# Taking GpSimd out of the attention stage of a bidirectional gated-recurrence and mixture-of-experts block

## The chip, the cores and the metric

The kernel runs on one core of a Trainium2 chip. A core has a matrix engine (TensorE, PE in the profile; PEld is its loading of weights), VectorE (DVE), ScalarE (ACT), GpSimd (POOL) and SyncE (SP), which here only issues transfers. Each engine works through its own list of instructions in order; the engines wait for each other by semaphores. The metric is the time of one execution on the device, in microseconds (us), as the median of several runs; lower is better.

## The reference

One block of a diffusion model works on 256 latent tokens and 256 context tokens, each 1024 wide, in fp32. Cut to what matters:

```
mod = silu(c) @ w_mod + b_mod               # 6 rows of 1024: sh1, sc1, g1, sh2, sc2, g2
h   = rms_norm(x) * (1 + sc1) + sh1         # the context gets rows of its own
q, i, f_fwd, f_bwd, og, u, v, ga, gb = split(h @ w_in)   # 9 sections of 1024
f   = lb + (1 - lb) * sigmoid(f_logit);  k = 1 - f
# gated recurrence, 8 heads x 128, forward and backward, in chunks of 64:
b   = cumsum(log f) in the chunk;  r = b[31];  e = b[63]
s_t = (q * exp(b - r)) . (k * exp(r - b)), masked
o   = s_t @ i + (q * exp(b)) @ S
S   = exp(e) * S + (k * exp(e - b))^T @ i
# S starts from the context:  S0 = sum_s (k * exp(tail))^T @ i,  tail = sum of log f behind s
y_a = rms_norm(o) * gnorm * silu(og)
y_b = chunk_mlp(gelu(u), gelu(v))
x   = x + g1 * ((sigmoid(ga) * (y_a @ w_a) + sigmoid(gb) * (y_b @ w_b)) @ w_out)
x   = x + g2 * top4_of_32_experts(rms_norm(x) * (1 + sc2) + sh2)
out = rms_norm(x) * final_g
```

## The kernel before

**Stages.** Up to about 60 us the kernel computes the first two modulation rows, normalizes the tokens and projects the values and both forget logits of the first two heads. From there to about 345 us runs the attention stage, with which the change deals: the remaining sections of the projection for the heads, and the recurrence. Then come the chunk MLP, the branch projections and the output projection (to some 490 us), and from there to the end the 32 experts, whose weights stream through the chip at over 400 GB/s.

**Projections.** They are done in fp32 by three matmuls: ScalarE writes the high part of a weight (`ghi`, L265), VectorE subtracts it (`glo`, L266), and TensorE adds high times high, high times low and low times high (L346, from `hh`, `hl`, `ghi`, `glo`). A granule of weights is 1024 x 256, one transfer of 1 MB.

**The ring.** Granules of `w_in` and the tiles of `w_mod` (1024 KB too: four rows of 128 times 512 columns) share three slots. SyncE's queue issues their transfers in order, and each waits until its slot is free.

**Modulation sums.** The rows `g1`, `sh2`, `sc2`, `g2` are needed only later. Each is computed in two halves of 512 columns (`mod_sums`, L206 to L229), each half in two steps: step 0 for the first four blocks of 128 rows of `w_mod`, step 1 for the other four. Step 0 was GpSimd's: one product of 128x2048 with the broadcast conditioning column (L215), a sum of 128x1024 (L216) and one of 128x512 (L221). Step 1 was and is VectorE's: four fused multiply-adds of 128x512 (L228). A matmul with ones then sums over the partitions (L248, tile `tp`).

**A head.** `decays` (L444 to L480) takes logarithms of the forget gates (ScalarE, L450), makes four scans on VectorE (L458: `bl` within chunks, `cu` over the context), the difference `d` to the chunk's middle (L467), and on ScalarE the exponentials: `e1` and `e2` of plus and minus `d`, `cu`, and the small tile `w` of chunk decays (L475). VectorE multiplies these to the queries (L477) and keys (L478, tile `lf`). GpSimd subtracted 1 from the context's gate (L452), set two elements of `cu` to zero (L455), copied the 16 columns that go into `w` (L470, L471) and multiplied the context's keys (L479). `states` makes the scores (L496, TensorE), masks them (VectorE), turns the keys (L506, copied by L507) and computes the chunks' sums U (L515 and L518, tiles `ua` and `ub`). `output` carries the states over the chunks: an addition (L529, VectorE) and a scaling by two columns (L530), forward on VectorE and backward on GpSimd, tile `ks`; then TensorE adds up the head's output (`o_ps`, L535 and L539). `finish` normalizes it (square sums on ScalarE; `rstd_of` on VectorE, L103 to L109, with the small tiles `nv`, `ni`, `ny`, `nt`; L553 writes `on`), turns it (L556, tile `tp` from `on`), multiplies it with the gate, and splits it into high and low.

**The order.** The heads go in pairs. While the projections of pair j run, the heads of pair j-1 are computed, interleaved as a string says:

```
ORDER = "x0 d0 y0 m0 d1 x1 m1 d2 x2 y1 x3 m2 d3 y2 m3 y3 d4"
```

Here `d0` to `d4` are the projections of pair j (values, silu of q, silu of the output gate, both forget gates), `x0` to `x3` and `y0` to `y3` are decays, states, output and finish of the two heads, and `m0` to `m3` are the steps of two halves of a modulation row (step 0 and step 1 of each). In the last round gates stand in the place of the projections. From the order so written the framework's scheduler makes each engine's list: it simulates a timeline with costs of its own and lets ready instructions go ahead, so an edit of one instruction's engine or size also moves others. The experts' part is ordered by hand and isn't touched.

Of the kernel before, what the change touches and what calls it, by code (L numbers as in the profile page):

```python
# [12 lines left out]
AF = mybir.ActivationFunctionType  # L13
OP = mybir.AluOpType
PSUM = bass.MemoryType.PSUM

P = 128
D = 1024
KT = 8
T = 256  # L20
# [6 lines left out]
def view(t, off, dims):  # L27
    return bass.AP(tensor=t.tensor, offset=t.offset + off, ap=[t.ap[0], *dims])
# [3 lines left out]
def kernel(  # L32
# [5 lines left out]
    ve, sc, te, gp = nc.vector, nc.scalar, nc.tensor, nc.gpsimd  # L38
# [120 lines left out]
    for h in range(2):  # L159
        b = slice(h * 64, h * 64 + 64)  # L160
# [41 lines left out]
    cs32 = late.tile([P, KT, 32], F32, name="cs32")  # L202
# [3 lines left out]
    def mod_sums(j, h):  # L206

        a = wk.tile([P, 512], F32, name="modrow")

        def step(k4):  # L210
            wt = wtile([P, 4, 512])
            nc.sync.dma_start(wt, w_mod[0, k4 * 512:(k4 + 1) * 512, j * D + h * 512:j * D + (h + 1) * 512]
                              .rearrange("(k p) n -> p k n", p=P))
            if k4 in MOD_POOL:
                gp.tensor_mul(wt, wt, cs32[:, 4 * k4:4 * k4 + 4, 0:1].to_broadcast([P, 4, 512]))  # L215
                gp.tensor_add(wt[:, 0:2], wt[:, 0:2], wt[:, 2:4])  # L216
                if k4:
                    gp.tensor_add(a, a, wt[:, 0])
                    gp.tensor_add(a, a, wt[:, 1])
                else:  # L220
                    gp.tensor_add(a, wt[:, 0], wt[:, 1])  # L221
            else:
                for q in range(4):
                    kt = 4 * k4 + q
                    if kt == 0:
                        ve.tensor_scalar(a, wt[:, q], cs32[:, kt, 0:1], None, op0=OP.mult)
                    else:
                        ve.scalar_tensor_tensor(a, wt[:, q], cs32[:, kt, 0:1], a, op0=OP.mult, op1=OP.add)  # L228
        return a, step  # L229

    def mod_col(j, h, res):
# [158 lines left out]
    for k in range(2):  # L390
        a, b = cols2[:, 8 + 16 * k:16 + 16 * k], cols2[:, 16 + 16 * k:24 + 16 * k]
# [51 lines left out]
    def decays(hd, k, q):  # L443


        col = slice(hd, hd + 1)
        lf = wk.tile([P, 2, 2 * T], F32, name="lf")
        tc.keep_in_program_order(sc.preload_act_table_set("natural_log_exp_and_others"))
        for dr in range(2):
            tc.keep_in_program_order(sc.activation(lf[:, dr], k[:, dr], AF.Ln, scale=omlb[dr][:, col], bias=lb[dr][:, col]))  # L450
        kl, kc = k[:, :, 0:T], k[:, :, T:2 * T]
        gp.tensor_scalar(kc, kc, -1.0, None, op0=OP.add)  # L452
        bl = wk.tile([P, 2, T], F32, name="bl")
        cu = wk.tile([P, 2, T], F32, name="cu")
        gp.memset(view(cu, T - 1, [[1, 2]]), 0.0)  # L455

        def scan(dst, o, src, so, m, n, st):
            ve.tensor_tensor_scan(view(dst, o, [[st, n]]), m, view(src, so, [[st, n]]), 0.0, op0=OP.mult, op1=OP.add)  # L458

        whole = view(reset, 1, [[0, T - 1]])  # L460
        scan(bl, 0, lf, 0, reset, T, 1)
        scan(bl, 2 * T - 1, lf, 3 * T - 1, reset, T, -1)
        scan(cu, T - 2, lf, 2 * T - 1, whole, T - 1, -1)
        scan(cu, T + 1, lf, 3 * T, whole, T - 1, 1)
        e1, e2 = lf[:, :, 0:T], lf[:, :, T:2 * T]
        d1 = wk.tile([P, 2, T], F32, name="d1")
        ve.tensor_sub(view(d1, 0, [[T, 2], [64, 4], [1, 64]]), view(bl, 0, [[T, 2], [64, 4], [1, 64]]),  # L467
                      view(bl, 31, [[T + 1, 2], [64, 4], [0, 64]]))
        w = wk.tile([P, 2, 2, 4], F32, name="w")
        gp.tensor_copy(w[:, 0], view(bl, 31, [[T + 1, 2], [64, 4]]))  # L470
        gp.tensor_copy(w[:, 1], view(d1, 63, [[T - 63, 2], [64, 4]]))  # L471
        sc.activation(e1, d1, AF.Exp)
        sc.activation(e2, d1, AF.Exp, scale=-1.0)
        sc.activation(cu, cu, AF.Exp)
        sc.activation(w, w, AF.Exp)  # L475
        for dr in range(2):
            ve.scalar_tensor_tensor(e1[:, dr], e1[:, dr], nomlb[dr][:, col], q, op0=OP.mult, op1=OP.mult)  # L477
        ve.scalar_tensor_tensor(e2, kl, -1.0, e2, op0=OP.add, op1=OP.mult)  # L478
        gp.tensor_mul(cu, cu, kc)  # L479
        return e1, e2, cu, w  # L480

    def attend(hd, dec, iv, og):
# [38 lines left out]
        def output():  # L521
            qt, w = dec[0], dec[3]
            sm, S, R, U, ua, ub = (st[k] for k in ("sm", "S", "R", "U", "ua", "ub"))
            sc.activation(S[:, 0, 0], ua[:, 3], AF.Copy, scale=w[:, 0, 0, 0:1])
            sc.activation(S[:, 1, 3], ub[:, 3], AF.Copy, scale=w[:, 0, 1, 3:4])
            for n in range(3):
                for dr, a, b in ((0, n, n + 1), (1, 3 - n, 2 - n)):
                    r = R[:, dr, b]
                    ve.tensor_add(r, S[:, dr, a], U[dr, a])  # L529
                    (gp if dr else ve).tensor_scalar(S[:, dr, b], r, w[:, 1, dr, a:a + 1], w[:, 0, dr, b:b + 1],  # L530
                                                     op0=OP.mult, op1=OP.mult)
            o = bank("o_ps", (P, 2, P))
            for tt in range(2):
                for dr in range(2):
# [518 lines left out]

ORDER = "x0 d0 y0 m0 d1 x1 m1 d2 x2 y1 x3 m2 d3 y2 m3 y3 d4"
FIRST = 6
MOD_POOL = (0,)
WARM = 20
WARM2 = (3, 12)
RING_A = 3
# [30 lines left out]
```

## Time and profile before

The rows are one profiled execution; the times are of runs without a profile.

| what | before |
|---|---|
| median of 3 runs | 1435.1 us |
| lowest and highest run | 1431.59 and 1438.36 us |
| profiled execution | 1439.14 us |
| its span | 1437.4 us |
| mean granted clock of TensorE | 0.978 |
| TensorE matmuls busy | 1341.1 us, 93% of the span |
| TensorE weight loads busy (beside matmuls) | 727.7 us, 51% |
| VectorE busy | 615.9 us, 43% |
| ScalarE busy | 306.2 us, 21% |
| GpSimd busy | 171.8 us, 12% |

The span is the time from the first to the last recorded instruction. Busy shares are averages over stages that differ, so a stage is read from rows for its own stretch of time. A row of the timeline begins with the start and the length of an instruction, both in us, then its engine, line, operation, result and sources, and behind x its number; in brackets stands the idle time of the engine just ahead of it, with what ended that. A row of the waits names who waited for whom: us in total, how often, and the longest. A row of a tile gives the shortest, middle and longest duration in ns. Granted clock 1.00 is TensorE's full speed.

### The profile page before, as it was taken

The page shows a single profiled execution, that of the slowest core. Times are in us where ns is not written, and L with a number is a line of the kernel's source. Part 1 is how long each engine was busy: PE and PEld are TensorE (multiplying, and loading weights), DVE is VectorE, ACT ScalarE, POOL GpSimd, SP SyncE. Part 2 cuts the span into 40 slices and gives each one's busy share as a digit, 9 for nine tenths or more (in the row PEclk, how much of TensorE's full clock was granted, in tenths as well). Part 3 has the DMA queues.
Part 4 walks back from the last instruction along what each step waited for, and adds up shares of the span by engine and source line. Part 5 has one row for each costly group of instructions (what it writes and reads, how often), then busy time and mean ns, then how long its engine had stood idle before and what let it go on. Part 6 is the DMA issues. An engine that isn't in the chain of part 4 may idle for free. (4 is left out here: it accounts for less than half of the span.)

```text
span 1437.4 us, 18504 instructions
## 1 busy us (share of the span) xinstructions
PE 1341.1 (93%) x7806; PEld 727.7 (51%) x7806; DVE 615.9 (43%) x1100; ACT 306.2 (21%) x494; POOL 171.8 (12%) x147
## 2 busy tenths in 40 slices
PE   6988898989999999999999999989999899898986
PEld 3887787788999843333333332323323233232322
DVE  5597777768768522322322323213222232222214
ACT  3472545365444310000000000000000000010001
POOL 3045434240064000000000000000000000000001
PEclk8999999999999999999999999999999999999998
DMA  9645252534984899999999999999999999999994
GB/s 333 193 147 173 98 200 92 173 125 162 325 256 175 344 418 411 427 424 425 425 424 427 427 424 426 423 428 426 425 426 423 427 426 426 425 424 426 426 424 156
DMA packets 106882, 487.37 MB, mean 339 GB/s; under 512 B 6277, under 2 KB 64778, under 8 KB 77098
## 3 DMA queue, kind: packets, MB, share of 16 engines
q1 hardware_dynamic: 105946, 483.37, 83.9%
q0 software_dynamic: 848, 2.75, 0.6%
q8 instruction: 63, 1.03, 0.3%
q14 instruction: 25, 0.20, 0.0%
HBM read 485.06 MB, written 1.05 MB: 338 GB/s over the span
## 5 line engine op out<-in xcount | busy, mean ns | idle before, releaser
L827 PE MATMUL gate<-w,xT 128*64 128x512 f32 x1024 | 269.1, 604 | 13.4 <-DMA w<-in_w_dram 13.0
L827 PE MATMUL lin<-w,xT 128*64 128x512 f32 x1024 | 263.0, 592 | 0.0
L864 PE MATMUL py<-w,hT 128*64 128x512 f32 x992 | 227.2, 605 | 26.0 <-DMA w<-in_w_dram 25.9
L883 DVE SCALAR_TENSOR_TENSOR acc<-sc,wts,acc 128x512 f32<-128x512 f32 x122 | 86.0, 747 | 206.1 <-PE sc L880 206.1
L346 PE MATMUL acc<-hh,glo 128*128 128x256 f32 (+1 forms) x480 | 150.1, 314 | 7.3 <-DVE glo L266 7.3
L864 PEld LDWEIGHTS py<-w,hT 128*64 128x64 f32 x992 | 70.5, 139 | 162.5 <-issue 115.2
L266 DVE TENSOR_TENSOR glo<-w,ghi 128x1024 fp32r<-128x1024 f32 (+1 forms) x99 | 130.4, 1321 | 50.0 <-ACT ghi L265 49.7
L346 PE MATMUL acc<-hh,ghi 128*128 128x256 f32 (+1 forms) x480 | 151.6, 316 | 0.0
L346 PE MATMUL acc<-hl,ghi 128*128 128x256 f32 (+1 forms) x480 | 149.8, 312 | 0.0
L827 PEld LDWEIGHTS lin<-w,xT 128*64 128x64 f32 x1024 | 73.1, 137 | 146.6 <-issue 146.6
L827 PEld LDWEIGHTS gate<-w,xT 128*64 128x64 f32 x1024 | 62.6, 136 | 152.1 <-issue 103.5
L265 ACT ACTIVATE ghi<-w 128x1024 fp32r<-128x1024 f32 (+1 forms) x102 | 102.5, 1009 | 140.4 <-PE acc L346 109.0
L962 POOL DMA_DIRECT2D bc<-in_final_g_dram x1 | 0.6, 559 | 893.5 <-PE misc L809 893.5
L867 DVE TENSOR_TENSOR y<-py,g2h 128x512 f32<-128x512 f32 x31 | 21.4, 692 | 192.1 <-PE py L864 192.1
L346 PEld LDWEIGHTS acc<-hh,glo 128*128 128x128 f32 x480 | 95.1, 198 | 12.3 <-DVE glo L266 7.8
L346 PEld LDWEIGHTS acc<-hh,ghi 128*128 128x128 f32 x480 | 94.9, 198 | 4.5 <-issue 0.8
L346 PEld LDWEIGHTS acc<-hl,ghi 128*128 128x128 f32 x480 | 94.9, 198 | 4.2 <-issue 0.4
L802 ACT ACTIVATE xT<-misc,sh,a 128x128 f32<-128x128 f32 (+1 forms) x68 | 30.7, 452 | 276.7 <-DVE xT L804 276.7
L804 DVE TENSOR_SCALAR xT<-misc,a,sh 128x128 f32<-128x128 f32 (+1 forms) x68 | 27.3, 401 | 134.3 <-PE misc L798 123.7
L834 DVE TENSOR_SCALAR g<-gate 128x512 f32<-128x512 f32 x32 | 22.1, 692 | 138.2 <-PE gate L827 138.2
L835 ACT ACTIVATE s<-g 128x512 f32<-128x512 f32 x32 | 20.2, 630 | 282.7 <-DVE g L834 282.7
L798 PEld LDWEIGHTS misc<-p,acc 128*128 128x128 f32 x544 | 66.6, 196 | 26.6 <-issue 26.0
(323 smaller groups left out, 1696.4 us busy)
## 6 DMA issues: line engine op xcount, KB each, us to landing
w<-in_w_dram SPq DMA_DIRECT2D x148, 2048.0 KB, 29.5
w<-in_w_dram SPq DMA_DIRECT2D x88, 1024.0 KB, 31.5
w<-in_w_in_dram SPq DMA_DIRECT2D x33, 1024.0 KB, 5.1
w<-in_w_mod_dram SPq DMA_DIRECT2D x24, 1024.0 KB, 5.2
w<-in_w_branch_b_dram SPq DMA_DIRECT2D x4, 1024.0 KB
w<-in_w_branch_a_dram SPq DMA_DIRECT2D x4, 1024.0 KB, 11.8
w<-in_w_out_dram SPq DMA_DIRECT2D x4, 1024.0 KB, 10.3
w<-in_w_in_dram SPq DMA_DIRECT2D x12, 256.0 KB, 9.3
```

The lines of the kernel that those rows point to most:

```text
L265: sc.activation(hi, src, AF.Copy)
L266: eng.tensor_sub(lo, src, hi)
L346: te.matmul(o, l, r, start=opens and kt == 0 and n == 0, stop=kt == KT - 1 and n == 2, skip_group_check=True)
L798: te.matmul(pg[:, k], view(x1, tt * D + kt // 2 * 256 + kt % 2, [[2, P]]), tok[:, tt], start=tt == 0, stop=tt == 1)
L802: sc.activation(xT[:, kt], pg[:, k], AF.Identity, bias=sh2[:, kt:kt + 1], scale=a2[:, kt:kt + 1])
L804: ve.tensor_scalar(xT[:, kt], pg[:, k], a2[:, kt:kt + 1], sh2[:, kt:kt + 1], op0=OP.mult, op1=OP.add)
L827: te.matmul(zz[n][h * C:(h + 1) * C], xT[:, kt], w[:, 0, n * D + h * 512:n * D + (h + 1) * 512], start=False, stop=kt == KT - 1, skip_grou ...
L834: ve.tensor_scalar(g, zz[0], 7.0, None, op0=OP.min)
L835: sc.activation(s, g, AF.Sigmoid, scale=1.702)
L864: te.matmul(py[h * C:(h + 1) * C], hT2[:, kt % 4, (kt // 4) * C:(kt // 4) * C + C], w[:, k, h * 512:(h + 1) * 512], start=False, stop=kt = ...
L867: ve.tensor_mul(y, py, g2h)
L883: ve.scalar_tensor_tensor(acc[:, tt, s], pcs[h], wcol[tt], old[:, tt, s], op0=OP.mult, op1=OP.add)
```

## The change

GpSimd gives up all its data work in the attention stage. The first halves of the modulation sums (step 0) become one multiplication and three fused multiply-adds on VectorE, as step 1 had them. The subtraction of 1 and the multiplication of the context's keys become one fused operation on VectorE (new L468). The zeros in `cu` and the backward scaling of the states go to VectorE (new L445 and L519). The two small copies into `w` go away: ScalarE's exponential reads the columns where they are, in two instructions instead of one (new L463 and L464).

```diff
--- before.py
+++ after.py
@@ -211,21 +211,12 @@
             wt = wtile([P, 4, 512])
             nc.sync.dma_start(wt, w_mod[0, k4 * 512:(k4 + 1) * 512, j * D + h * 512:j * D + (h + 1) * 512]
                               .rearrange("(k p) n -> p k n", p=P))
-            if k4 in MOD_POOL:
-                gp.tensor_mul(wt, wt, cs32[:, 4 * k4:4 * k4 + 4, 0:1].to_broadcast([P, 4, 512]))
-                gp.tensor_add(wt[:, 0:2], wt[:, 0:2], wt[:, 2:4])
-                if k4:
-                    gp.tensor_add(a, a, wt[:, 0])
-                    gp.tensor_add(a, a, wt[:, 1])
+            for q in range(4):
+                kt = 4 * k4 + q
+                if kt == 0:
+                    ve.tensor_scalar(a, wt[:, q], cs32[:, kt, 0:1], None, op0=OP.mult)
                 else:
-                    gp.tensor_add(a, wt[:, 0], wt[:, 1])
-            else:
-                for q in range(4):
-                    kt = 4 * k4 + q
-                    if kt == 0:
-                        ve.tensor_scalar(a, wt[:, q], cs32[:, kt, 0:1], None, op0=OP.mult)
-                    else:
-                        ve.scalar_tensor_tensor(a, wt[:, q], cs32[:, kt, 0:1], a, op0=OP.mult, op1=OP.add)
+                    ve.scalar_tensor_tensor(a, wt[:, q], cs32[:, kt, 0:1], a, op0=OP.mult, op1=OP.add)
         return a, step
 
     def mod_col(j, h, res):
@@ -449,10 +440,9 @@
         for dr in range(2):
             tc.keep_in_program_order(sc.activation(lf[:, dr], k[:, dr], AF.Ln, scale=omlb[dr][:, col], bias=lb[dr][:, col]))
         kl, kc = k[:, :, 0:T], k[:, :, T:2 * T]
-        gp.tensor_scalar(kc, kc, -1.0, None, op0=OP.add)
         bl = wk.tile([P, 2, T], F32, name="bl")
         cu = wk.tile([P, 2, T], F32, name="cu")
-        gp.memset(view(cu, T - 1, [[1, 2]]), 0.0)
+        ve.memset(view(cu, T - 1, [[1, 2]]), 0.0)
 
         def scan(dst, o, src, so, m, n, st):
             ve.tensor_tensor_scan(view(dst, o, [[st, n]]), m, view(src, so, [[st, n]]), 0.0, op0=OP.mult, op1=OP.add)
@@ -467,16 +457,15 @@
         ve.tensor_sub(view(d1, 0, [[T, 2], [64, 4], [1, 64]]), view(bl, 0, [[T, 2], [64, 4], [1, 64]]),
                       view(bl, 31, [[T + 1, 2], [64, 4], [0, 64]]))
         w = wk.tile([P, 2, 2, 4], F32, name="w")
-        gp.tensor_copy(w[:, 0], view(bl, 31, [[T + 1, 2], [64, 4]]))
-        gp.tensor_copy(w[:, 1], view(d1, 63, [[T - 63, 2], [64, 4]]))
         sc.activation(e1, d1, AF.Exp)
         sc.activation(e2, d1, AF.Exp, scale=-1.0)
         sc.activation(cu, cu, AF.Exp)
-        sc.activation(w, w, AF.Exp)
+        sc.activation(w[:, 0], view(bl, 31, [[T + 1, 2], [64, 4]]), AF.Exp)
+        sc.activation(w[:, 1], view(d1, 63, [[T - 63, 2], [64, 4]]), AF.Exp)
         for dr in range(2):
             ve.scalar_tensor_tensor(e1[:, dr], e1[:, dr], nomlb[dr][:, col], q, op0=OP.mult, op1=OP.mult)
         ve.scalar_tensor_tensor(e2, kl, -1.0, e2, op0=OP.add, op1=OP.mult)
-        gp.tensor_mul(cu, cu, kc)
+        ve.scalar_tensor_tensor(cu, kc, -1.0, cu, op0=OP.add, op1=OP.mult)
         return e1, e2, cu, w
 
     def attend(hd, dec, iv, og):
@@ -527,8 +516,7 @@
                 for dr, a, b in ((0, n, n + 1), (1, 3 - n, 2 - n)):
                     r = R[:, dr, b]
                     ve.tensor_add(r, S[:, dr, a], U[dr, a])
-                    (gp if dr else ve).tensor_scalar(S[:, dr, b], r, w[:, 1, dr, a:a + 1], w[:, 0, dr, b:b + 1],
-                                                     op0=OP.mult, op1=OP.mult)
+                    ve.tensor_scalar(S[:, dr, b], r, w[:, 1, dr, a:a + 1], w[:, 0, dr, b:b + 1], op0=OP.mult, op1=OP.mult)
             o = bank("o_ps", (P, 2, P))
             for tt in range(2):
                 for dr in range(2):
@@ -1053,7 +1041,6 @@
 
 ORDER = "x0 d0 y0 m0 d1 x1 m1 d2 x2 y1 x3 m2 d3 y2 m3 y3 d4"
 FIRST = 6
-MOD_POOL = (0,)
 WARM = 20
 WARM2 = (3, 12)
 RING_A = 3
```

Lines have moved up by 9 to 13 in the new kernel. GpSimd's list shrinks from 122 rows to 52, with nothing left between the start-up and the loading of the experts' biases. ScalarE's table loads are 29, 28 before. On SyncE's queue one load of `w_branch_a` now stands ahead of two of `w_in` and four of `w_branch_b`.

VectorE's list in the third group of heads (heads 2 and 3, between the difference `d` of the first head and its keys `lf<-sg`, which the scores wait for) before: the second head's scans and the first head's queries (`lf<-lf,lbn,q`), the difference of the second, then the keys.

```order
L467 TENSOR_TENSOR d_1568<-bl 128x512
L458 SCALAR_TENSOR_TENSOR bl<-attc,lf 128x256
L458 SCALAR_TENSOR_TENSOR cu<-attc,lf 128x255
L266 TENSOR_TENSOR ylo<-y,yhi 128x256
L458 SCALAR_TENSOR_TENSOR bl<-attc,lf 128x256
L458 SCALAR_TENSOR_TENSOR cu<-attc,lf 128x255
L477 SCALAR_TENSOR_TENSOR lf<-lf,lbn_722,q 128x256
L477 SCALAR_TENSOR_TENSOR lf<-lf,lbn_736,q 128x256
L467 TENSOR_TENSOR d_1703<-bl 128x512
L478 SCALAR_TENSOR_TENSOR lf<-sg_911,lf 128x2x256
```

The same place now (`cu<-sg,cu` is the fused multiplication of the context's keys, `nv` and `ni` are steps of a norm's root, `glo` is the low part of projection weights):

```order
L457 TENSOR_TENSOR d_1565<-bl 128x512
L448 SCALAR_TENSOR_TENSOR bl<-attc,lf 128x256
L448 SCALAR_TENSOR_TENSOR cu<-attc,lf 128x255
L103 TENSOR_SCALAR nv<-ss 128x2
L468 SCALAR_TENSOR_TENSOR cu<-sg_911,cu 128x512
L457 TENSOR_TENSOR d_1698<-bl 128x512
L104 TENSOR_SCALAR ni<-nv 128x2
L257 TENSOR_TENSOR glo<-w,ghi 128x1024
L466 SCALAR_TENSOR_TENSOR lf<-lf,lbn_722,q 128x256
L466 SCALAR_TENSOR_TENSOR lf<-lf,lbn_736,q 128x256
L467 SCALAR_TENSOR_TENSOR lf<-sg_911,lf 128x2x256
```

Two of the second head's scans and a split of y have moved ahead of the first head's `d`, as has a row of the modulation sums (L219, between the scans ahead of these rows); the context's keys, a weight split and two small steps of a norm have come in ahead of the keys. On TensorE the scores that wait for these keys stand behind 720 matmuls of the projections, counted from the beginning; before it was 672.

TensorE's list at the end of the attention stage, before (`acc` are projection matmuls, `tp<-ident,on` turns a normalized output, `tp<-modrow,ones` sums a modulation row, `o_ps` is the last head's output). These rows stand behind the last head's sums U (`ua`, `ub`) and 23 projection matmuls that follow them; 26 more projection matmuls stand ahead of the sums:

```order
L346 MATMUL acc<-ghi,hh 128x256
L346 MATMUL acc<-ghi,hl 128x256
L556 MATMUL tp<-ident,on 128x128
L248 MATMUL tp<-modrow,ones 128x512
L556 MATMUL tp<-ident,on 128x128
L535 MATMUL o_ps<-iv,attc 128x128 x2
L539 MATMUL o_ps<-ks,lf 64x128 x2
L346 MATMUL acc<-glo,hh 128x256
```

The same place now, where `ub<-wr_sb,sh` is a product of the router's weights with a modulation row:

```order
L507 MATMUL ua<-iv,ks 128x128 x2
L507 MATMUL ub<-iv,ks 128x128 x2
L544 MATMUL tp<-ident,on 128x128
L239 MATMUL tp<-modrow,ones 128x512
L544 MATMUL tp<-ident,on 128x128
L523 MATMUL o_ps<-iv,attc 128x128 x2
L527 MATMUL o_ps<-ks,lf 64x128 x2
L674 MATMUL ub<-wr_sb,sh_71 128x32 x8
L527 MATMUL o_ps<-ks,lf 64x128 x2
```

The 49 projection matmuls that stood around the last head's sums now come ahead of them, and between the sums and the other head's turned output there is no other work.

## The prediction

> **What bounds the kernel now.** I first cut the span into its stages (windows), then asked who made TensorE wait in the stage that the change touches (waits), then read the instructions around the longest of these waits in order of time (timeline), and last the price of single operations (groups by tile).
>
> The span, and the three stages (each row: length, busy us of an engine with its number of instructions, granted clock, DMA share, GB/s):
>
> ```profile
> span 1437.4 us, 18504 instructions
> ```
>
> ```profile
> core 0: us, PE busy (x) PEld busy (x) DVE busy (x) ACT busy (x) POOL busy (x), PEclk, DMA share, GB/s
> 60.00:340.00 280.00, 250.45 (x1921) 220.90 (x1920) 215.46 (x357) 140.40 (x218) 112.59 (x83) 0.94 0.46 154
> 340.00:490.00 150.00, 149.07 (x1280) 146.47 (x1279) 109.20 (x151) 67.94 (x95) 41.20 (x31) 1.00 0.73 239
> 490.00:1430.00 940.00, 893.89 (x4267) 326.50 (x4266) 256.98 (x496) 77.71 (x150) 4.47 (x5) 0.99 0.99 416
> ```
>
> From 490 us on the experts are bound by transfers (DMA share 0.99), and their bytes don't change. From 340 to 490 TensorE is busy 149.07 of 150 us at full clock. From 60 to 340, where the change lies, TensorE is idle for 29.5 us, and its clock is 0.94, which costs 280 x 0.06 = 16.8 us more. So 46.3 us can be won there at most. What is won goes through to the end: the ring's slots, and so the transfers of the experts, are freed by TensorE's progress, and 0.73 leaves the DMA room before them.
>
> Who ended TensorE's waits in that stage (us in total, times, longest):
>
> ```profile
> PE scores L496 <- DVE lf L478: 13.2, 3, 7.0
> PE acc L346 <- DVE glo L266: 7.3, 2, 3.8
> PE tp L556 <- DVE on L553: 5.0, 2, 2.6
> PE ua L518 <- ACT ks L507: 2.0, 1, 2.0
> PE acc L346 <- DVE q L420: 1.0, 1, 1.0
> PE acc L346 <- DVE og L420: 1.0, 1, 1.0
> ```
>
> These six rows are 29.5 us, all of the idle time, and 27.5 of it ends on VectorE. Why VectorE is late shows in time. In this stretch (third group of heads) TensorE is idle for 6.0 of 15 us, because the scores wait for their keys (L478, which ends at 176.5):
>
> ```profile
> 162.00:177.00 15.00, 8.97 (x85) 8.69 (x84) 14.10 (x15) 8.16 (x14) 13.70 (x10) 0.90 0.00 0
> ```
>
> GpSimd there, then VectorE (start, us):
>
> ```profile
> 161.30 3.69 POOL L215 TENSOR_TENSOR w<-w,cs 128x2048 f32<-128x2048 f32 x1 [17.72 <-DMA w<-in_w_mod_dram]
> ...
> 167.60 2.89 POOL L216 TENSOR_TENSOR w<-w 128x1024 f32<-128x1024 f32 x1
> ```
>
> ```profile
> 160.28 1.23 DVE L266 TENSOR_TENSOR glo<-w,ghi 128x1024 fp32r<-128x1024 f32 x1 [0.16 <-ACT ghi L265]
> 162.90 2.62 DVE L458 TENSOR_TENSOR_SCAN bl<-attc,lf 128x256 f32<-128x256 f32 x1 [1.39 <-ACT lf L450]
> 165.45 1.03 DVE L458 TENSOR_TENSOR_SCAN cu<-attc,lf 128x255 f32<-128x255 f32 x1
> 166.40 0.66 DVE L458 TENSOR_TENSOR_SCAN bl<-attc,lf 128x256 f32<-128x256 f32 x1
> ...
> 168.15 2.89 DVE L458 TENSOR_TENSOR_SCAN bl<-attc,lf 128x256 f32<-128x256 f32 x1
> ...
> 173.41 1.86 DVE L477 SCALAR_TENSOR_TENSOR lf<-lf,lbn,q 128x256 f32<-128x256 f32 x2
> ...
> 175.79 0.68 DVE L478 SCALAR_TENSOR_TENSOR lf<-sg,lf 128x512 f32<-128x512 f32 x1
> ```
>
> The same scan takes 0.66 us by itself and 2.62 or 2.89 while GpSimd multiplies or adds: VectorE's instruction ends when GpSimd's does. The groups by tile (min/median/max ns) say that this is general:
>
> ```profile
> L458 DVE TENSOR_TENSOR_SCAN bl<-attc,lf x16: 658/692/2893, 76.6 to 316.5; 128x256 f32<-128x256 f32 x16
> L467 DVE TENSOR_TENSOR d<-bl x8: 658/660/4028, 79.3 to 318.0; 128x512 f32<-128x512 f32 x8
> L108 DVE SCALAR_TENSOR_TENSOR nt<-nt,nv x21: 160/161/3565, 135.6 to 341.7; 128x2 f32<-128x2 f32 x21
> L477 DVE SCALAR_TENSOR_TENSOR lf<-lf,lbn,q x16: 454/474/1509, 91.3 to 325.4; 128x256 f32<-128x256 f32 x16
> ```
>
> Even an operation on 128x2 (nt, a step of the norm's root) has once taken 3.565 us.
>
> **The change, part by part.** GpSimd loses all its 112.59 us in this stage. VectorE gets 24 multiply-adds and 8 multiplies of modulation rows, 8 fused multiplies of context keys, 24 scalings of states and 8 tiny memsets; ScalarE splits one exponential into two. The prices:
>
> ```profile
> L228 DVE SCALAR_TENSOR_TENSOR modrow<-w,cs,modrow x32: 733/750/753, 100.2 to 331.1; 128x512 f32<-128x512 f32 x32
> L478 DVE SCALAR_TENSOR_TENSOR lf<-sg,lf x8: 673/679/1755, 84.6 to 325.8; 128x512 f32<-128x512 f32 x8
> L530 DVE TENSOR_SCALAR ks<-ks,w x22: 328/342/625, 119.6 to 343.2; 128x128 f32<-128x128 f32 x22
> L475 ACT ACTIVATE w<-w 128x16 f32<-128x16 f32 x8 | 1.5, 206 | 0.0
> ```
>
> 24 x 0.75 = 18.0, 8 multiplies of 128x512 between 0.34 (the scaling of 128x128) and 0.75 (I take 0.5) = 4.0, 8 x 0.68 = 5.4, 24 x 0.34 = 8.2: 35.6 us go onto VectorE, and below 0.5 us of memsets. ScalarE, busy for half of the stage, gets 8 x 0.2 = 1.6 us and by its order one more table load; its row is of 1283 ns:
>
> ```profile
> L448 ACT ACT_TABLE_LOAD x8 | 10.3, 1283 | 0.1
> ```
>
> Both at nothing, since none of the six waits but the one of 2.0 ends on ScalarE (without that cover 2.9). On SyncE's queue one load of a branch weight moved ahead of six others behind the stage, at nothing too: 0.73 there leaves room (5 us if it didn't, a transfer's time, below). VectorE stood at 215.46 of 280, so the 35.6 alone would make it 251, near its bound; but the excess over the median goes too, 2.2 us in the longest scan, 3.4 in d and in nt each, and so on. For this row the Trainium skill speaks against the change: the "Vector Engine (DVE) Microarchitecture Reference", section "Points that are easy to get wrong", says that a scalar-tensor-tensor with two non-bf16 SBUF sources runs at half throughput. The trace does not show it: L478 with two such sources has a median of 679 ns against 660 for the plain two-input d of the same size; by the rule the 32 fused operations would add 32 x 0.66 = 21 us, and VectorE's 35.6 would be 57.
>
> Now wait by wait. *Scores (13.2).* From 162.9 on, the excess over undisturbed operations is 1.9 + 0.4 + 2.2 in scans and 1.86 - 0.95 = 0.9 in L477: 5.4 us. What now stands there is in the order shown with the change (VectorE, third group, from the first head's d to its keys). The keys now stand behind a fused multiply (0.68), a weight split (glo, 1.2) and, ahead of these rows, a modulation row (0.75): 2.6 us put in, 5.4 taken out. TensorE's order moved too: 720 projection matmuls come before these scores, 672 before; 48 x 149.07/1280 = 5.6 us of cover. This wait goes. In the fourth group one score stays behind 960 matmuls as before, with the same 5.4 out and some 3 in: of 7.0 I leave 3.0. *Splits (7.3).* The split waits behind these:
>
> ```profile
> 79.32 4.03 DVE L467 TENSOR_TENSOR d<-bl 128x512 f32<-128x512 f32 x1
> ```
>
> ```profile
> 302.76 2.63 DVE L458 TENSOR_TENSOR_SCAN bl<-attc,lf 128x256 f32<-128x256 f32 x1 [1.39 <-ACT lf L450]
> 305.31 1.03 DVE L458 TENSOR_TENSOR_SCAN cu<-attc,lf 128x255 f32<-128x255 f32 x1
> 306.26 0.66 DVE L458 TENSOR_TENSOR_SCAN bl<-attc,lf 128x256 f32<-128x256 f32 x1
> 306.85 2.79 DVE L458 TENSOR_TENSOR_SCAN cu<-attc,lf 128x255 f32<-128x255 f32 x1
> ```
>
> d falls from 4.03 to 0.66 and one multiply (0.5) comes in: 0.4 of the 3.5 is left, since 3.4 went. The four scans lose 4.5 and three modulation rows (2.2) come in: of 3.8 I leave 1.5. Together 1.9. *Norms (5.0)* are nt and its like under GpSimd: none left. *ScalarE's copy (2.0)* I leave; q and og (1.0 each) go. Of 29.5 us 6.9 are left: 22.6 won.
>
> *Clock.* TensorE's clock halves behind the waits, behind the one of 2.0 us too:
>
> ```profile
> 115.90:119.30 3.40, 3.40 (x17) 3.40 (x18) 3.36 (x6) 0.74 (x2) 1.11 (x1) 0.50 0.31 93
> 276.30:279.70 3.40, 3.40 (x10) 2.63 (x9) 2.35 (x9) 1.47 (x2) 1.30 (x2) 0.50 0.92 308
> ```
>
> Two waits that I leave cost 1.7 us each in this way, so 16.8 - 3.4 = 13.4 are won. The Trainium skill's "TensorE: Matmul & The Clock Gate", Part 1, wants an idle window of about 3.4 us before it throttles; by that rule these two would cost nothing, and the time would be 3.4 us lower. The rows of 2.0 and 2.6 us speak against it.
>
> *The tail.* In the order of TensorE shown with the change, 23 projection matmuls stood between the states of the last head (U, in ua and ub) and the other head's turned output (tp from on), and 26 more ahead of those states; now none stands there. Nothing covers the root of that head's norm and the other's chain of states. The price lies between 0 and the cover that is gone, 49 x 0.116 = 5.7; I take 4 (the wait at L556 was 2.6 at most, but with cover) and 1.7 of clock: 5.7 lost.
>
> *New waits on VectorE.* A modulation row now waits for its transfer in VectorE's queue, with scans and splits behind it:
>
> ```profile
> POOL w L215 <- DMA w<-in_w_mod_dram: 46.5, 5, 17.7
> ```
>
> ```profile
> DVE modrow L228 <- DMA w<-in_w_mod_dram: 3.5, 3, 1.9
> ```
>
> The price lies between 0 and 46.5; GpSimd was simply early, VectorE's own rows waited 3.5 for as many loads, so I take 3. For a wait that I can't name I set one of the list's size, 3.8.
>
> Sum: 22.6 + 13.4 - 5.7 - 3 - 3.8 = 23.5 us. The profiled execution took 1439.1 (its span and 1.7 around it), which would become 1415.6; the median of the runs is 4.0 lower, 1435.1, so 1411.6: **1411**.
>
> **The rivals.** (1) *VectorE stays the late one*: its 35.6 us fall into the same chains. Half of the 22.6 comes (11.3), no clock, the tail costs 5.7: 5.6 won, 1429. For it: VectorE is on every row of the waits but one. Against: the excess that goes is about as large. (2) *Slower: VectorE queues behind transfers.* At each of the 8 first halves of a modulation load VectorE waits for a landing, which takes
>
> ```profile
> w<-in_w_mod_dram SPq DMA_DIRECT2D x24, 1024.0 KB, 5.2
> ```
>
> 5.2 us, and TensorE with it, plus 1.7 of clock: 55.2 us in place of 46.3, so 1444. It decides from 46.3/8 = 5.8 us a load. The 46.5 speak for it, the 3.5 against. (3) *All is cured*: 46.3 won with neither tail nor new waits, 1389; for it that the order gives TensorE later scores everywhere. That GpSimd would still hold VectorE can't be: nothing is left on it.
>
> **How the numbers follow.** Forecast 0.6 (1400 to 1423), rival 1 0.2, rival 2 0.07, rival 3 0.13. The range 1393 to 1431 leaves out rival 2 and the ends of 1 and 3. A measurement can tell 0.5% (7.2 us) from no change. Faster by more: forecast, rival 3 and the lower third of rival 1, 0.8; within: 0.13; slower: 0.07.
>
> **What would show it.** Right: in the stage behind 60 us scans at 0.66 to 0.69 throughout, no nt over 0.2, waits of scores and splits under 5 us in total, clock at 0.97 or more, a wait of 2 to 5 us at the turned outputs at the stage's end. Wrong: long scans with GpSimd idle; modulation rows that wait for transfers for more than 15 us; or the same stage shorter and the experts' start not earlier.

## The result, and the profile after

The changed kernel takes 1410.05 us (median of 4 runs, 1408.96 to 1414.03) against 1434.68 (4 runs, one more than ahead of the prediction, 1431.59 to 1438.36): a ratio of 0.9832, 95% interval 0.9802 to 0.9863, or 24.6 us less. Its profiled execution took 1408.96 us, 30.2 less than that of before. The profiled execution of before was 4.5 us over the median of its runs, that of after 1.1 below: that is the difference between 30.2 and 24.6. What follows accounts for the 30.2.

The span, and the same three stages as before the change (length, busy us of each engine with instructions, granted clock, DMA share, GB/s):

```profile
span 1407.2 us, 18450 instructions
```

```profile
core 0: us, PE busy (x) PEld busy (x) DVE busy (x) ACT busy (x) POOL busy (x), PEclk, DMA share, GB/s
60.00:340.00 280.00, 270.15 (x2163) 237.68 (x2162) 215.06 (x480) 152.31 (x242) 0.00 (x0) 0.99 0.50 166
340.00:490.00 150.00, 148.39 (x1192) 134.91 (x1191) 101.45 (x155) 62.66 (x88) 40.40 (x28) 1.00 0.85 298
490.00:1430.00 940.00, 865.20 (x4108) 311.67 (x4108) 247.72 (x452) 72.12 (x139) 4.48 (x5) 0.99 0.96 405
```

In the attention stage TensorE does 2163 matmuls where it did 1921, with its clock at 0.99 in place of 0.94. VectorE is busy for 215.06 us where it was for 215.46, but the fixed window now also holds work that stood behind 340 us before. From 60 us to the chunk MLP VectorE is busy for 224.7 us against 244.1: it lost more in stretched instructions than it got in new ones. The first product of the chunk MLP starts at 352.3 us (378.6 before) and the first expert at 466.3 (494.6).

All waits of TensorE in the stage, 60 to 345 us (total, times, longest):

```profile
PE acc L337 <- ACT v L623: 2.4, 1, 2.4
PE tp L544 <- DVE on L541: 2.2, 1, 2.2
PE acc L337 <- ACT iv L422: 1.9, 1, 1.9
PE ua L504 <- DVE ks L496: 1.3, 1, 1.3
PE acc L337 <- ACT mb L564: 0.8, 1, 0.8
PE acc L337 <- DVE og L411: 0.5, 1, 0.5
PE o_ps L527 <- DVE ks L519: 0.4, 1, 0.4
PE acc L337 <- DVE q L411: 0.2, 1, 0.2
```

9.7 us are left of 29.5. The scores (13.2) and the weight splits (7.3) are gone from the list. The scans and the differences by tile (shortest, median, longest in ns):

```profile
L448 DVE TENSOR_TENSOR_SCAN bl<-attc,lf x16: 658/681/692, 76.2 to 279.7; 128x256 f32<-128x256 f32 x16
L457 DVE TENSOR_TENSOR d<-bl x8: 658/684/686, 78.9 to 280.9; 128x512 f32<-128x512 f32 x8
```

No scan is over 692 ns (2893 before), no difference over 686 (4028), and no `nt` over 164 (3565).

### The profile page after: what moved, and what is told of

Read it like the earlier page. It is cut to its first block, busy times and chain, and to the rows that moved or that the text cites. A ratio compares the mean times of both kernels' runs of the same rounds, so it can differ in the third digit from the quotient of the medians.

```text
span 1407.2 us, 18450 instructions
## 1 busy us (share of the span) xinstructions
PE 1331.7 (95%) x7806; PEld 718.5 (51%) x7806; DVE 596.4 (42%) x1176; ACT 306.3 (22%) x499; POOL 58.3 (4%) x59
## 5 line engine op out<-in xcount | busy, mean ns | idle before, releaser
L337 PE MATMUL acc<-hh,ghi 128*128 128x256 f32 (+1 forms) x480 | 147.3, 307 | 2.7 <-ACT iv L422 1.9
L337 PE MATMUL acc<-hh,glo 128*128 128x256 f32 (+1 forms) x480 | 145.1, 303 | 0.2
L337 PE MATMUL acc<-hl,ghi 128*128 128x256 f32 (+1 forms) x480 | 145.2, 303 | 0.0
L257 DVE TENSOR_TENSOR glo<-w,ghi 128x1024 fp32r<-128x1024 f32 (+1 forms) x99 | 126.8, 1286 | 40.3 <-ACT ghi L256 40.1
L337 PEld LDWEIGHTS acc<-hh,ghi 128*128 128x128 f32 x480 | 90.1, 188 | 8.0 <-ACT iv L422 2.1
L337 PEld LDWEIGHTS acc<-hh,glo 128*128 128x128 f32 x480 | 90.0, 188 | 4.6 <-DVE glo L257 0.6
L337 PEld LDWEIGHTS acc<-hl,ghi 128*128 128x128 f32 x480 | 90.2, 188 | 3.9 <-issue 0.6
L337 PE MATMUL acc<-ghi,hh 128*128 128x256 f32 x256 | 73.3, 287 | 9.3 <-ACT hh L256 6.2
## 6 DMA issues: line engine op xcount, KB each, us to landing
w<-in_w_dram SPq DMA_DIRECT2D x148, 2048.0 KB, 29.5
w<-in_w_branch_b_dram SPq DMA_DIRECT2D x4, 1024.0 KB, 13.4
```

The costliest lines, as they stand in the source:

```text
L257: eng.tensor_sub(lo, src, hi)
L337: te.matmul(o, l, r, start=opens and kt == 0 and n == 0, stop=kt == KT - 1 and n == 2, skip_group_check=True)
```

## The experiments

Three theories were set against each other, and a fourth is added below. *Hold*: GpSimd's instructions keep VectorE's from running, VectorE is late for that reason, and TensorE waits for it. *Order*: what helps is the other order, in which TensorE's scores stand behind more projection work. *Chain*: GpSimd's slow steps in a head's own chain were late. The ratios are to the kernel before on the same chip; its medians on these chips lie between 1434.7 and 1436.8, so differences of 2 us between the times of two rows can be those of the chips. "Excess" is summed over VectorE's instructions in the stage that overlap one of GpSimd's: their length less the median of the undisturbed ones of the same kind. "Idle" is TensorE's idle time from 72 us to the chunk MLP; the last column is the start of that MLP's first weight load.

| kernel | us | ratio to before (95%) | excess | idle | MLP at |
|---|---|---|---|---|---|
| before | 1434.7 | | 47.7 | 29.4 | 378.5 |
| after | 1410.05 | 0.9832 (0.9802 to 0.9863) | 0.0 | 9.8 | 352.2 |
| modulation sums alone | 1408.54 | 0.9815 (0.9792 to 0.9839) | 11.1 | 10.0 | 345.3 |
| the rest alone | 1434.24 | 0.9995 (0.9983 to 1.0007) | 43.1 | 25.3 | 372.5 |
| before, light modulation | 1413.40 | 0.9856 (0.9835 to 0.9878) | 9.8 | 14.8 | 353.3 |
| after, release only | 1412.74 | 0.9847 (0.9820 to 0.9875) | 0.0 | 11.6 | 351.4 |
| half the idle product | 1426.19 | 0.9942 (0.9919 to 0.9964) | 17.6 | 18.1 | 369.4 |
| idle product | 1447.19 | 1.0075 (1.0053 to 1.0098) | 36.8 | 37.4 | 390.6 |
| idle one-input work | 1418.78 | 0.9882 (0.9859 to 0.9905) | 10.1 | 16.5 | 359.8 |
| after, backward scaling back | 1405.14 | 0.9790 (0.9767 to 0.9812) | 0.7 | 6.6 | 346.4 |
| after, all scaling on GpSimd | 1403.45 | 0.9774 (0.9747 to 0.9802) | 0.2 | 6.9 | 344.5 |
| after, other last order | 1411.99 | 0.9845 (0.9821 to 0.9869) | 0.0 | 9.5 | 352.8 |
| after, light VectorE | 1404.99 | 0.9789 (0.9766 to 0.9812) | 0.0 | 5.0 | 343.4 |

**The modulation sums alone.** The kernel before, with one line changed:

```diff
-MOD_POOL = (0,)
+MOD_POOL = ()
```

> Only the modulation sums go to VectorE; the heads' small work stays on GpSimd. Three theories. Hold: GpSimd's instructions with two inputs keep VectorE's instructions from ending, and what the change removes is this. By the trace of before, the three modulation instructions (product, two sums) account for 38 of some 47 us by which VectorE's instructions are over their undisturbed lengths in the attention stage. So this part brings about 38/47 of the 24.6 us: 20, time 1415 (1410 to 1420), and VectorE's excess in the stage is near 9 us. Order: what helps is that TensorE's scores now stand behind more projection matmuls (720 and 1008 here for the third and fourth group, 672 and 960 before): also about 1410 to 1415, so this run can't tell it from the first. Chain: GpSimd's slow steps inside a head's chain (context keys, scaling of states) were what was late: nothing gained, 1430 or more.

1408.54: just below what hold and order gave, and no slower than the whole change. Chain falls: GpSimd's small steps are all still there.

```profile
60.00:340.00 280.00, 269.75 (x2198) 239.78 (x2197) 219.62 (x447) 156.68 (x242) 55.10 (x62) 1.00 0.53 172
```

GpSimd is busy for 55.10 us in the stage and TensorE's clock is 1.00.

**The rest alone.** The kernel after, with the modulation sums of before:

```diff
-            for q in range(4):
-                kt = 4 * k4 + q
...
+            if k4 in MOD_POOL:
+                gp.tensor_mul(wt, wt, cs32[:, 4 * k4:4 * k4 + 4, 0:1].to_broadcast([P, 4, 512]))
+                gp.tensor_add(wt[:, 0:2], wt[:, 0:2], wt[:, 2:4])
...
+MOD_POOL = (0,)
```

> Only the heads' small work (context keys, state scaling, small copies) goes to VectorE and ScalarE; the modulation sums stay on GpSimd. TensorE's scores stand behind 720 and 1008 projection matmuls here, as in the kernel after the change or later. Hold: 38 of 47 us of VectorE's excess stay, so 1425 to 1432, with scans and steps of the norm's root at 2.6 us and more while GpSimd multiplies or adds. Order: 1410 to 1415. Chain: 1410 to 1415.

1434.24, no gain that can be measured, though the scores stand behind 720 and 1008 projection matmuls. Order and chain give 1410 to 1415 here; both fall. The time is 2 us over what hold gave. In the third group GpSimd, then VectorE, then ScalarE (start, length; in brackets the idle time ahead):

```profile
157.42 3.61 POOL L215 TENSOR_TENSOR w<-w,cs 128x2048 f32<-128x2048 f32 x1 [21.32 <-DMA w<-in_w_mod_dram]
161.11 2.66 POOL L216 TENSOR_TENSOR w<-w 128x1024 f32<-128x1024 f32 x1
163.85 1.53 POOL L221 TENSOR_TENSOR modrow<-w 128x512 f32<-128x512 f32 x1
```

```profile
157.75 3.83 DVE L457 TENSOR_TENSOR_SCAN bl<-attc,lf 128x256 f32<-128x256 f32 x1
161.50 2.81 DVE L457 TENSOR_TENSOR_SCAN cu<-attc,lf 128x255 f32<-128x255 f32 x1
164.24 1.70 DVE L457 TENSOR_TENSOR_SCAN bl<-attc,lf 128x256 f32<-128x256 f32 x1
165.86 0.66 DVE L457 TENSOR_TENSOR_SCAN cu<-attc,lf 128x255 f32<-128x255 f32 x1
```

```profile
161.62 0.22 ACT L472 ACTIVATE w<-bl 128x8 f32<-128x8 f32 x1 [3.04 <-DVE bl L457]
164.35 0.63 ACT L471 ACTIVATE cu<-cu 128x512 f32<-128x512 f32 x1 [2.52 <-DVE cu L457]
...
167.19 0.63 ACT L469 ACTIVATE lf<-d 128x512 f32<-128x512 f32 x1 [1.26 <-DVE d L466]
...
168.98 0.56 ACT L431 COPY iv<-acc 128x512 f32<-128x512 f32 x1
```

Three scans in a row, one for each of GpSimd's three instructions, each ending 0.5 to 0.6 us behind it, about an undisturbed scan's length: the scan runs when GpSimd is done. ScalarE's exponentials wait for the scans, and behind them in ScalarE's queue stands the copy of the values (iv) that frees TensorE's accumulators. So TensorE's wait is put down to ScalarE:

```profile
PE acc L346 <- ACT iv L431: 10.0, 2, 5.7
```

With the new order no wait for the scores is left (13.2 before), but 10.0 us at this copy and 10.0 at the weight splits (7.3 before) have come in their place.

**The kernel before with light modulation sums.** GpSimd's three instructions on 8 of 512 columns; the rest of each first half is left out:

```diff
-                gp.tensor_mul(wt, wt, cs32[:, 4 * k4:4 * k4 + 4, 0:1].to_broadcast([P, 4, 512]))
-                gp.tensor_add(wt[:, 0:2], wt[:, 0:2], wt[:, 2:4])
+                gp.tensor_mul(wt[:, :, 0:8], wt[:, :, 0:8], cs32[:, 4 * k4:4 * k4 + 4, 0:1].to_broadcast([P, 4, 8]))
+                gp.tensor_add(wt[:, 0:2, 0:8], wt[:, 0:2, 0:8], wt[:, 2:4, 0:8])
...
-                    gp.tensor_add(a, wt[:, 0], wt[:, 1])
+                    gp.memset(a, 0.0)
+                    gp.tensor_add(a[:, 0:8], wt[:, 0, 0:8], wt[:, 1, 0:8])
```

> The kernel before, with GpSimd's three modulation instructions cut to 8 of 512 columns (the rest of each first half is left out and set to zero, so the modulation sums lack that part). Nothing is added to VectorE, the heads' small work stays on GpSimd, and TensorE's scores stand behind 672 and 960 projection matmuls as in the kernel before. Hold: 38 of 47 us of VectorE's excess go, and with no work added: 1405 to 1415. Order: the scores stand where they stood, 1428 to 1435. Chain: as before, 1430 to 1435.

1413.40. With the scores where they stood before, 21 us are won (the whole change won 24.6) as the excess falls from 47.7 to 9.8 us. The score waits left are 8.3 us:

```profile
PE scores L497 <- DVE lf L479: 8.3, 3, 3.2
```

A fourth theory, *ring*, would explain this run too: GpSimd's late last sum keeps a slot of the ring, and so a transfer, waiting. SyncE's queue waits for that sum (L221) for 47.8 us in the stage before, for 8.3 here. The next run tells ring from hold, because its GpSimd work holds no slot.

**Idle work with two inputs on GpSimd.** The kernel after, with work that nothing reads, behind the first multiplication of each first half:

```diff
                     ve.tensor_scalar(a, wt[:, q], cs32[:, kt, 0:1], None, op0=OP.mult)
+                    ve.tensor_copy(scr[:, 0, 0:1], wt[:, 0, 0:1])
+                    for _ in range(2):
+                        gp.tensor_mul(scr, scr, cs32[:, 0:2, 0:1].to_broadcast([P, 2, 512]))
+                    gp.tensor_add(scr, scr, scr)
+                    gp.tensor_add(scr[:, 0], scr[:, 0], scr[:, 1])
...
```

> The kernel after the change, with work on GpSimd that nothing reads: at each of the 8 first halves of a modulation load it does two products of 128x1024, one sum of 128x1024 and one of 128x512 on a scratch tile of its own, released by a copy of one column on VectorE. Order of all other instructions on TensorE, ScalarE and SyncE as after the change. Nothing waits for GpSimd by a semaphore. Hold: VectorE's instructions get longer again, 30 to 40 us in total in the stage, and the time goes to 1420 to 1430. Order and chain: nothing happens, 1410 within 0.3%.

1447.19: the direction of hold, and 17 us more than its upper end. Apart from the release copies and a memset that changed places with its neighbour, the engines' order is that of after, and nothing, SyncE's queue included, waits for GpSimd; so ring falls with order and chain. GpSimd, then VectorE, in the third group:

```profile
156.95 5.24 POOL L220 TENSOR_TENSOR scr<-scr,cs 128x1024 f32<-128x1024 f32 x2 [16.71 <-DVE scr L218]
162.28 2.22 POOL L221 TENSOR_TENSOR scr<-scr 128x1024 f32<-128x1024 f32 x1
164.57 1.52 POOL L222 TENSOR_TENSOR scr<-scr 128x512 f32<-128x512 f32 x1
```

```profile
157.52 2.92 DVE L262 TENSOR_TENSOR glo<-w,ghi 128x1024 fp32r<-128x1024 f32 x1
160.36 2.38 DVE L224 SCALAR_TENSOR_TENSOR modrow<-w,cs,modrow 128x512 f32<-128x512 f32 x1
162.67 2.38 DVE L455 TENSOR_TENSOR_SCAN bl<-attc,lf 128x256 f32<-128x256 f32 x1
164.97 1.68 DVE L455 TENSOR_TENSOR_SCAN cu<-attc,lf 128x255 f32<-128x255 f32 x1
166.57 0.72 DVE L224 SCALAR_TENSOR_TENSOR modrow<-w,cs,modrow 128x512 f32<-128x512 f32 x1
```

Undisturbed the first four take 1.22, 0.75, 0.68 and 0.66 us. GpSimd is done at 166.1, and the multiply-add at 166.57 is back at its undisturbed length.

**Half of it, and none of it.** The idle product for only one of each row's two halves, and only the copies that release it:

```diff
+                    if h == 0:
+                        for _ in range(2):
...
```

> As the idle product, at 4 of the 8 places only. If each held instruction costs by itself, the excess is near 18 us and the time half way between 1410 and 1447: 1426 to 1431. If the loss only sets in when VectorE has no room left, it is less than half: 1412 to 1422.

> The control of the idle works: the scratch tile and the 8 copies of one column on VectorE that release them, without work on GpSimd behind. All theories: 1410, within 0.3%.

1426.19 and 1412.74. From none over 17.6 to 36.8 us of excess the time grows by 13.5 and by 34.5: 0.8 and 0.9 us per us. The half is at the lower edge of what was expected if each held instruction costs by itself, and 4 us above the other expectation. The interval of the control holds the 0.9832 of after. Why a us of excess costs 0.8 to 0.9 here and 0.57 in the order of before (21.5 us for 37.9, the light modulation sums) stays open.

**Idle work with one input.** In the place of products and sums:

```diff
+                    for _ in range(2):
+                        gp.tensor_scalar(scr, scr, cs32[:, 0, 0:1], None, op0=OP.mult)
...
```

> As the idle product, but GpSimd's idle work is two one-input multiplications by a column (128x1024 each) at each of the 8 places, on the same scratch tile and with the same release. If any data instruction of GpSimd holds VectorE, it costs like the idle product by its GpSimd time: 1425 to 1447. If only those with two inputs do (in the trace before, 14.3 us of the one-input state scaling go with 0.1 us of excess on VectorE, 14.6 us of the one-input subtraction of 1 with 3.0), the excess stays under 8 us and the time at 1410 to 1414. If lateness on GpSimd's queue is what counts in the idle product, the two cost the same.

1418.78, between the two expectations: neither holds. GpSimd's work is 56.1 us long, the idle product's 68.9, but the excess is 10.1 against 36.8, and the loss against the control 6.0 us against 34.5. GpSimd and VectorE in the third group:

```profile
148.17 8.20 POOL L220 TENSOR_SCALAR scr<-scr,cs 128x1024 f32<-128x1024 f32 x2 [16.87 <-DVE scr L218]
```

```profile
149.85 1.53 DVE L222 SCALAR_TENSOR_TENSOR modrow<-w,cs,modrow 128x512 f32<-128x512 f32 x1
151.30 0.68 DVE L453 TENSOR_TENSOR_SCAN bl<-attc,lf 128x256 f32<-128x256 f32 x1
151.90 0.66 DVE L453 TENSOR_TENSOR_SCAN cu<-attc,lf 128x255 f32<-128x255 f32 x1
152.48 0.72 DVE L222 SCALAR_TENSOR_TENSOR modrow<-w,cs,modrow 128x512 f32<-128x512 f32 x1
153.13 0.68 DVE L453 TENSOR_TENSOR_SCAN bl<-attc,lf 128x256 f32<-128x256 f32 x1
153.73 1.45 DVE L453 TENSOR_TENSOR_SCAN cu<-attc,lf 128x255 f32<-128x255 f32 x1
```

Eleven of VectorE's instructions overlap GpSimd's 8.2 us; six of them are shown, with the only two that are held, for 0.8 us each.

**The scaling of the states given back**, the backward one, then both:

```diff
-                    ve.tensor_scalar(S[:, dr, b], r, w[:, 1, dr, a:a + 1], w[:, 0, dr, b:b + 1], op0=OP.mult, op1=OP.mult)
+                    (gp if dr else ve).tensor_scalar(S[:, dr, b], r, w[:, 1, dr, a:a + 1], w[:, 0, dr, b:b + 1], op0=OP.mult, op1=OP.mult)
```

> The kernel after the change, with the backward scaling of the states given back to GpSimd (24 instructions of 128x128; one input). VectorE is rid of 8 us. The order at the end of the attention stage comes out with 24 projection matmuls behind the last head's sums and 26 ahead, as before the change. Hold (two-input instructions only): no excess to speak of, and the 5 us of the end (two waits and a slow clock) go: 1403 to 1408. If one-input instructions hold too, or GpSimd's longer scaling (635 ns against 342) lengthens the chain of states: 1410 to 1416.

> The kernel after the change with all 48 scalings of states on GpSimd, forward and backward (24 of them were VectorE's before the change too): VectorE is rid of 16 us, GpSimd has some 30 us of one-input work, and both directions wait for each other in its queue. If VectorE's load is what still costs: 1402 to 1405. If the chain of states becomes longer (two scalings of 0.6 us in a row in place of one of 0.34 beside another) and TensorE's head outputs wait for it: 1406 to 1412, with waits of o_ps on GpSimd's ks.

1405.14 and 1403.45: both within the first of their expectations. These instructions, of 0.6 us on GpSimd, hold nothing to speak of (excess 0.7 and 0.2 us). With both, TensorE waits for the chain of states for 3.0 us in all:

```profile
PE o_ps L527 <- POOL ks L519: 3.0, 2, 1.6
```

That is less than what is won elsewhere. Both kernels beat before. Every run of either is also below every run of after (1407.28 at most, against 1408.96), but these ran on other chips, and the intervals of the ratios still touch that of after. Between the two the intervals overlap.

**Another order for the last round.**

```diff
+LAST = "x0 d0 y0 x1 d1 y1 d2 x2 y2 x3 y3 d3 m0 m1 m2 m3 d4"
...
-            for step in ORDER.split():
+            for step in (ORDER if j < 4 else LAST).split():
```

> The kernel after the change, with another written order for the last round alone (x0 d0 y0 x1 d1 y1 d2 x2 y2 x3 y3 d3, then the modulation steps, d4): 25 projection matmuls ahead of the last head's sums and 23 behind them, in place of none. The tail term of the prediction (two waits of 1.3 and 2.2 us and 1.7 us of clock in the trace after) goes: 1404 to 1407. If these matmuls are only missing elsewhere, the wait comes up at another place and the time is 1410 within 3 us.

1411.99: the second expectation holds. The waits at the turned output and at the sums U are gone from the list, and another stands at its head:

```profile
PE acc L337 <- ACT ghi L256: 2.6, 1, 2.6
```

**Less work on VectorE.** The kernel after with the first half of each sum on 8 of 512 columns; the rest is left out:

```diff
+            n = 512 if k4 else 8
...
-                    ve.tensor_scalar(a, wt[:, q], cs32[:, kt, 0:1], None, op0=OP.mult)
+                    ve.tensor_scalar(a[:, 0:n], wt[:, q, 0:n], cs32[:, kt, 0:1], None, op0=OP.mult)
...
```

> The kernel after the change, with VectorE's first half of each modulation sum cut to 8 of 512 columns (the rest is left out and is zero): VectorE has some 20 us less to do in the stage, GpSimd has nothing. If VectorE's added work costs TensorE nothing: 1408 to 1412, up to 5 us less where the order covers the end of the stage. If it falls into the chains that bound the stage (the first rival): 1398 to 1403.

1404.99: 5 us less than after for some 20 us less on VectorE. That lies within the proviso of the first expectation (up to 5 us less where the order covers the end), above the second; no wait at the end of the stage is left here. The order of the rows differs much too, so this run alone doesn't tell VectorE's load from the order.

## Why the prediction was right

The time fell by the mechanism that the forecast of 1411 named, and all the signs that it gave for being right are there. That it was met within 1 us is luck. Its sum of 23.5 us was taken off the profiled execution and gave 1415.6 there; the profiled execution after took 1408.96, 30.2 less. It fits the medians, which differ by 24.6, because the profile before lay 4.5 us above its median and that of after 1.1 below. Idle time (11.8 net forecast, 19.6 measured) was priced too low, and clock (11.7 net, 10.6) a little too high.

- **The bound and the cause.** Right, and shown (only that the held instruction ends 0.5 to 0.6 us behind GpSimd's, not with it): excess put back costs time in step with its amount (the idle products), and excess taken out of nearly the order of before brings 21 us (light modulation sums).
- **The cost of VectorE's new work, 35.6 us.** Right in size. The rows of after:

```profile
L219 DVE SCALAR_TENSOR_TENSOR modrow<-w,cs,modrow 128x512 f32<-128x512 f32 x56 | 41.8, 746 | 6.7 <-DMA w<-in_w_mod_dram 6.2
L217 DVE TENSOR_SCALAR modrow<-w,cs 128x512 f32<-128x512 f32 x8 | 3.8, 479 | 8.7 <-DMA w<-in_w_mod_dram 8.7
L468 DVE SCALAR_TENSOR_TENSOR cu<-sg,cu 128x512 f32<-128x512 f32 x8 | 5.5, 683 | 1.2 <-ACT cu L462 1.2
L519 DVE TENSOR_SCALAR ks<-ks,w 128x128 f32<-128x128 f32 x48 | 14.9, 341 | 0.1
```

24 x 0.746 + 3.8 + 5.5 + 24 x 0.341 = 35.4. The rule of the Trainium skill's "Vector Engine (DVE) Microarchitecture Reference", section "Points that are easy to get wrong", that a fused operation with two such sources runs at half rate, weighed in the prediction, is not seen in L468 either: 683 ns, where d takes 684.

- **Waits, 22.6 won.** Scores 13.2 to none, splits 7.3 to none on this list. The prediction had left 3.0 and 1.9, and by its own figures it should have left 4.6 (7.0 - 5.4 + 3) and 2.1 (3.5 - 3.4 + 0.5, and 1.5); both were too much. Norms 5.0 to none but the one at the tail, q and og 2.0 to 0.7. ScalarE's copy ahead of U, 2.0, is no longer late; U now waits 1.3 for VectorE's copy, at the tail.
- **The tail, 5.7 lost.** Waits of 1.3 and 2.2 and a half-clock stretch of 3.4 us, 5.2 in all. As a price of the order it was mistaken: with cover put back there the time stays the same (other last order), and a wait of 2.6 us has come up at another place.
- **New waits, 3 and 3.8 lost.** VectorE waits for modulation transfers by 6.2 and 8.7 us, as the rows above say, and never for more than 3.5 at once, below the 5.8 from which the second rival was to decide. Together they are 14.9, just under the 15 that the prediction named as a sign of being wrong. That sign would have misled: with the modulation sums alone they are 18.9 and with the backward scaling given back 19.7, in kernels that are no slower. Another wait on VectorE was not foreseen, 3.5 us of the memset in `cu` for TensorE's reading. No wait of TensorE on the list ends at either. The wait without a name came: 5.1 us on ScalarE (v, iv, mb) and 1.7 of clock, 6.8 us, as much as the two terms together, which is a coincidence, since they were set for other waits.
- **Clock, 13.4 won.** Mis-sized, as was the bound of 46.3: it counted twice the time in which TensorE was idle and its clock low. A row of before, inside the longest wait of the third group:

```profile
174.00:176.40 2.40, 0.00 (x0) 0.00 (x0) 2.40 (x4) 1.12 (x3) 1.45 (x2) 0.50 0.00 0
```

Here and in two other waits 6.2 of the 34.1 us at half clock hold no matmul. So (34.1 - 6.2)/2 = 14.0 us were lost, 3.4 are left, 1.7 at the tail and 1.7 at the waits without a name, and 10.6 were won. The prediction had left 5.1, the tail's 1.7 among them; whether a wait of 2 us costs its 1.7 at all was chance (the last section).

Idle 29.4 - 9.8 = 19.6 and clock 10.6 make 30.2. The chunk MLP starts only 26.3 earlier: the router's product of 1.9 us has moved ahead of it, and some 2 us these counts don't find. The rest came behind it: 2.0 us to the experts, of them the 1.9, and 1.9 in the experts, which no part of the change touches. So it is in part chance that the two counts make up the whole difference.

What the prediction did not separate is which part of the change does this. The modulation sums bring all of it. The rest brings nothing that can be measured, although with the sums alone 11.1 us of excess are left; and with the scaling of the states given back the kernel is 5 to 7 us faster by these times. This and the light VectorE speak for a part of the first rival (VectorE's own work in the same chains), and the other last order says that cover at the stage's end alone doesn't bring it; but in each of these kernels the order moved too, so the size of that part is not shown. The later place of the scores, to which the prediction gave 5.6 us of cover, does not help while the hold lasts: the rest alone has its scores as late or later and keeps 25.3 us of idle time.

## What to carry to other kernels

Look for instructions of one engine that are long only while another engine works, by the shortest and the longest of a group; a slow helper off the critical path can be what makes the engine on it slow. Not all work was worth moving off GpSimd here: the two-input products and sums over many columns were, the one-input scalings of 128x128, which held next to nothing, most likely not. And a wait that is covered in one place is often only moved, so cover is priced by a run, not by its row.

## What the runs showed of the hardware

**Which instructions are held.** In the trace of the idle product, of 39 VectorE instructions with all sources in SBUF, the working memory, that overlapped GpSimd's idle work 28 took at least 20% longer than undisturbed. Twelve with a source in PSUM, where TensorE's results lie (turned keys, q, og, y, the additions of U and others) overlapped it, and none took longer. Held were instructions with one input too: a multiplication of a modulation row by a column in 3 of 4 cases. The Trainium skill's "GPSIMD Engine Reference", section "Key points", says that GpSimd shares its SBUF interfaces with VectorE and contends with instructions in a two-port mode or with two SBUF inputs. The trace agrees for the most part in which are held. Beside 68.9 us of GpSimd's two-input forms the excess was 36.8 us, beside 56.1 us of the one-input form 10.1.

**The clock.** The same two waits of TensorE at the end of the stage, 2.2 and 2.4 us, cost half-clock stretches in the kernel after and none in the control with the release copies. Two rows of after:

```profile
317.10:320.50 3.40, 3.40 (x12) 1.91 (x11) 2.45 (x9) 0.14 (x1) 0.00 (x0) 0.50 0.02 5
327.30:330.70 3.40, 3.40 (x18) 3.40 (x17) 2.62 (x12) 0.03 (x1) 0.00 (x0) 0.50 0.00 0
```

The control, over both waits:

```profile
308.00:345.00 37.00, 31.05 (x266) 28.42 (x266) 24.05 (x72) 14.20 (x25) 0.00 (x0) 1.00 0.35 113
```

The clock records of the traces say why. Within each trace the half-clock stretches begin whole multiples of 3.413 us apart (before at 85.14, 115.86, 139.75, 173.88 us and on; in the control, outside the stage, at 17.61, 468.17, 495.47 us and on), and but for the one at the trace's end they last whole windows of that length. Where the windows lie differs from trace to trace. Cut along them, the thirteen traces have 1092 windows at full clock from 60 us to just behind the start of the chunk MLP. In 1059 of them TensorE is idle for 1.77 us at most, and the next window has full clock; in the other 33 it is idle for 1.59 us or more, and the next has half. In the kernel after each of the two waits lies whole in one window (2.20 and 2.44 us idle); in the control the windows cut them, into 1.77 and 0.45 and into 0.79 and 1.64. So in these traces about half a window of idle time was enough, and a wait of 2 us cost clock or not by where it fell.

The Trainium skill's "TensorE: Matmul & The Clock Gate", Part 1, has the activity window run freely, without regard to the kernel's start. The traces agree: the first such boundary behind the first instruction's start lies at another place in each of them (3.2 us before, 0.5 in the control).
